# LayerNorm's channel sums in a decoder block: GpSimd in place of TensorE, with six pairs of weight low parts on VectorE

## The chip, the core and the metric

The kernel runs on one core of a Trainium2 chip. The metric is device time in microseconds (us); three runs of the kernel before gave 786.52, 786.67 and 786.81 us.

The core has five engines, each working through a queue of its own in order: TensorE (PE in the profile; PEld is its weight load), VectorE (DVE), ScalarE (ACT), GpSimd (POOL) and SyncE (SP, which here only starts DMA transfers). They wait for each other through semaphores.

## The reference

One decoder block, batch 1, 512 positions, 1024 channels, float32. Two token mixers run side by side and a SwiGLU channel mixer follows. The part that matters here is the convolution branch with its LayerNorm, and what stands beside it:

```python
def layernorm(x, g, b):
    mu = jnp.mean(xf, axis=-1, keepdims=True)
    xc = xf - mu
    var = jnp.mean(xc * xc, axis=-1, keepdims=True)
    return xc * lax.rsqrt(var + EPS) * g + b
...
z_glu, z_rx, z_rg, z_ga, z_gb = jnp.split(h @ w_in[l] + b_in[l], split_idx, axis=-1)
u = z_glu[..., :D_CONV] * jax.nn.sigmoid(z_glu[..., D_CONV:])
u = causal_depthwise_conv(u, conv_dw_w[l], conv_dw_b[l])          # 31 taps
u = jax.nn.silu(layernorm(u, conv_ln_g[l], conv_ln_b[l]))
y_a = u @ conv_w_out[l] + conv_b_out[l]
...
y_b = (hb * jax.nn.gelu(z_rg, approximate=True)) @ lru_w_out[l]
m = jax.nn.sigmoid(z_ga) * y_a + jax.nn.sigmoid(z_gb) * y_b
x = x + m @ w_mix_out[l]
```

LayerNorm needs two sums over the 1024 channels for each of the 512 positions: one for the mean, one for the variance.

## The kernel before, in words

**Layout and products.** Activations lie channel by channel on the 128 partitions with the 512 positions along the row, so 1024 channels are 8 tiles of 128x512. A product of float32 matrices is made from two parts of each operand: a high part in the narrower type `fp32r` (a cast on ACT, line 126) and a low part, the rest (a subtraction, line 122). `mm3` (line 621) adds high x high, high x low and low x high, so that each weight tile costs three matmuls.

**Weights.** `wchunk` lists the weight pieces in the order in which PE wants them. A piece is loaded by SP into one of 8 raw buffers, cast by ACT, and its low part is made by the engine named by the argument `lo`: GpSimd (`pool_e`) by default, VectorE (`vec`) for some. High and low part go into one of 5 buffers (`hl`), which come free when PE is done with the piece five places earlier. The matrix `lru_w_out` comes as 16 pieces of 128x640, two for each of 8 output tiles (`lo0_0`, `lo0_1`, up to `lo7_1`); all low parts of these are on GpSimd. PE uses them in the stage that I call the `yb` stage (8 output tiles, 30 matmuls each), after the products with `w_in` (`z`) and ahead of those with `conv_w_out` (`ya`, which reads the normalised `un0` to `un7`).

**Order.** Most of the program is in the engines' queues in an order that the code writes itself (`tc.manual_schedule`). Small steps of VectorE work are dealt out beside the matmuls: generators such as `conv_lane` (the 31 taps, line 874) and `conv_norm` (LayerNorm) yield after each step, and `run_beside` takes so many steps of them for each output tile of PE. `MEAN_LAG` and `LAG` are counts of such steps that `conv_norm` lets pass between the two halves of a sum, so that the engines that make it have time.

**LayerNorm before.** The convolution lanes add the 8 tiles into `lnmt` (line 879). `conv_norm` splits this into a high part (`lnmsh`, ACT) and a low part (`lnmsl`, VectorE). `column_mean` (line 891) multiplies each by a 128x128 matrix of ones on PE, which leaves the sum over partitions on all partitions, and ACT scales it (line 892, `lnmp`, in PSUM). VectorE subtracts it from the 8 tiles (`u<-u,lnmp`), ACT squares them (line 906), VectorE adds the squares into `lnvt` (line 909, in PSUM), and the same split and products follow (`lnvsh`, `lnvsl`, `lnvp`). ACT takes the root (line 916), VectorE the reciprocal (line 917), then 8 products `u<-u,lnvp` (line 921), Silu on ACT (line 923), and the split into `un`.

**Other work in that place.** `mixq.make_sums` (tiles `mxws`, lines 113 and 344) prepares sums of quarters of `w_mix_out` on VectorE. `make_f_sums` does the same for pieces of the feed-forward weights: 12 pieces (`fws`), each loaded, added up by four GpSimd additions (line 114) and stored to DRAM (line 442, from GpSimd's queue for the last four).

Of the kernel before, what the change touches and what calls it, by code (L numbers as in the profile page):

```python
# [1 line left out]

# [5 lines left out]

# [2 lines left out]
AF = mybir.ActivationFunctionType  # L11
ALU = mybir.AluOpType

P = 128
T = 512
D = 1024
DC = 1024
# [20 lines left out]
PACK = HB // 2  # L38
ROWS_G = HB + PACK

MEAN_LAG, LAG = 9, 7
LANE_IN, LANE_OUT, XB_LAG, STEP_ROOM, LOAD_AHEAD, GATE_LAG = 3, 0, 1, 8.3, 2, 2


# [11 lines left out]
SUMS_AT, SUMS_STEP, SUMS_LAG, STORE_LAG = 3, 5, 2, 2  # L56
STORED_LAG = 3
SUMS_OWN = 40


MIX_LATE_LAG, LATE_LAG = 2, 8
# [23 lines left out]
def tile_block(ctx, tc, a, out):  # L85
# [8 lines left out]
    def tiles(tag, bufs):  # L94
        p_ = pool(tag, bufs)
        return lambda name, dtype=F32: p_.tile([P, T], dtype, tag=tag, name=name)

    longt, shortt = tiles("long", SLOTS), tiles("short", SHORT)

    def pairt(name, dtype=F32R):  # L100

        return longt(f"{name}h", dtype), longt(f"{name}l", dtype)

    def bank(name):
        return psum.tile([P, T], F32, tag="mm", name=name)

    def bank2(name):
        return psum2.tile([P, T], F32, tag="cv", name=name)

    vec, act, pe, pool_e = nc.vector, nc.scalar, nc.tensor, nc.gpsimd  # L110
# [5 lines left out]
    newest = {}  # L116
# [4 lines left out]
    def sub(eng, o, x, y):  # L121
        return eng.tensor_tensor(out=o, in0=x, in1=y, op=ALU.subtract)  # L122

    def split_to(h, l, full, eng, copy=act.copy):

        copy(h, full)  # L126
        if eng is None:
            put_off.append((l, full, h.bitcast(F32)))
            return h, l
        last = sub(eng, l, full, h.bitcast(F32))  # L130
        newest["sub" if eng is pool_e else "low"] = last.ins
        return h, l
# [17 lines left out]
    def split(name, full, eng, p_=None, copy=act.copy):  # L150
        p_ = p_ or pairt(name)
        return split_to(*p_, full, eng, copy)
# [7 lines left out]
    def wchunk(key, src, kt, cols, where="hl", lo=pool_e, after=None):  # L160
        chunks.append((key, src, kt, cols, where, lo, after))
# [87 lines left out]
    ORDER = """u0 u1 rx0 rx1 gb0 rx2 u2 gb1 h0 rx3 h1 h2 u3 rx4 h3 u4 h4 gb2 h5 rx5 h6 rg0 rx6 h7 u5 rx7 h8 gb3 rg1 rg2 rx8 h9 h10 rg3 gb4 u6 h11 rx9 h12 u7 h13 gb5 rg4 rg5 rg6 ga0 gb6 h14 ga1 gb7 ga2 rg7 h15 ga3 rg8 ga4 ga5 rg9 ga6 ga7""".split()  # L249
    ORDER = [(t.rstrip("0123456789"), int(t.lstrip("abcdefghijklmnopqrstuvwxyz"))) for t in ORDER]  # L250
# [9 lines left out]
    lru_out = a["lru_w_out"][0].rearrange("(k p) n -> p k n", p=P)  # L260
    for j in range(8):
        for hf in range(2):
            wchunk(f"lo{j}_{hf}", lru_out[:, 5 * hf : 5 * hf + 5, j * P : (j + 1) * P], 5, P)
    conv_out = a["conv_w_out"][0].rearrange("(k p) n -> p k n", p=P)
    for j in [0, 4, 1, 5, 2, 6, 3, 7]:
        wchunk(f"co{j}", conv_out[:, :, j * P : (j + 1) * P], ND, P, lo=vec)
# [158 lines left out]
    def piece_load(name, halves, queue=nc.sync):  # L425
        raw = raws.tile([P, 1024], F32, tag="raw", name=f"fws{name}")
        n = 1024 // len(halves)
        for h, src in enumerate(halves):
            queue.dma_start(raw[:, h * n : h * n + n].rearrange("p (e n) -> p e n", n=256), src)
        return raw  # L430

    def piece_sums(raw, dest, eng):
        of = raw.rearrange("p (h k e n) -> p h e k n", h=2, k=2, e=2)
        q11, q12, q21, q22 = (of[:, h, e] for h in range(2) for e in range(2))
        plus_on(eng, q22, q22, q12)
        plus_on(eng, q12, q12, q11)
        plus_on(eng, q11, q22, q11)
        plus_on(eng, q21, q21, q11)

    def piece_store(raw, dest, queue=nc.sync):  # L440
        dest = dest.rearrange("p m k n -> p (m k) n")
        return queue.dma_start(dest, raw.rearrange("p (m n) -> p m n", n=256))

    def make_f_sums():

        todo = list(f_todo)  # L450
        sums_due, stores_due = [], []
        n, next_at, stored = 0, SUMS_AT, [-9]
        while todo or sums_due or stores_due:
            if stores_due and (emitted[0] >= stores_due[0][0] or not (todo or sums_due)):
                stores_due.pop(0)[1]()
                stored[0] = n
            if sums_due and n >= sums_due[0][0]:
                sums_due.pop(0)[1]()
            if todo and n >= next_at and len(sums_due) + len(stores_due) + (n < stored[0] + STORED_LAG) < PIECES:
                next_at += SUMS_STEP  # L460
                name, halves, dest = todo.pop(0)
                with tc.issue_after(newest["load"]):
                    raw = piece_load(name, halves)

                def sums(raw=raw, dest=dest, own=n >= SUMS_OWN):
                    with tc.issue_after(newest["sub"]):
                        piece_sums(raw, dest, pool_e)
                        if own:
                            piece_store(raw, dest, pool_e)
                            return  # L470

                    def stores():
                        with tc.issue_after(newest["load"]):
                            piece_store(raw, dest)

                    stores_due.append((emitted[0] + STORE_LAG, stores))

                sums_due.append((n + SUMS_LAG, sums))
            n += 1
            yield  # L480
# [90 lines left out]
    eps_t = consts.tile([P, 1], F32, name="eps_t")  # L571
# [11 lines left out]
    onesr = consts.tile([P, P], F32R, name="onesr")  # L583
# [24 lines left out]
    def pc(name, i):  # L608
        return par[:, col[name] + i : col[name] + i + 1]
# [249 lines left out]
    ended, total = [], []  # L859
# [24 lines left out]
            act.copy(u[c], acc)  # L884
            yield False

    def column_mean(name, tot, scale):

        ps = bank2(f"{name}p")
        for i, v in enumerate(tot):  # L890
            pe.matmul(ps, onesr, v, start=i == 0, stop=i == 1)  # L891
        act.activation(ps, ps, AF.Copy, scale=scale)
        return ps

    def conv_norm():
        tot = split("lnms", total[0], vec)
        yield True
        for _ in range(MEAN_LAG):
            yield True
        mean = column_mean("lnm", tot, 1.0 / DC)  # L900
        yield True
        tot = bank2("lnvt")
        for c in range(8):
            sub(vec, u[c], u[c], mean)
            q = tot if c == 0 else shortt(f"sq{c}")
            act.activation(q, u[c], AF.Square)
            yield True
            if c:
                vec.tensor_tensor(out=tot, in0=tot, in1=q, op=ALU.add)
                yield True  # L910
        tot = split("lnvs", tot, vec)
        yield True
        for _ in range(LAG):
            yield True
        rs = column_mean("lnv", tot, 1.0 / DC)
        act.activation(rs, rs, AF.Sqrt, bias=eps_t)
        vec.reciprocal(rs, rs)
        for _ in range(6):
            yield True
        for c in range(8):  # L920
            vec.tensor_tensor(out=u[c], in0=u[c], in1=rs, op=ALU.mult)
            yield True
            act.activation(u[c], u[c], AF.Silu, scale=pc("conv_ln_g", c), bias=pc("conv_ln_b", c))
            un.append(split(f"un{c}", u[c], vec))
            yield True

    lanes += [conv_lane(0), conv_lane(1)]
    norm = conv_norm()

    def beside_one():  # L930
# [254 lines left out]
    for j in range(8):  # L1185
        ws = w_tiles(f"lo{j}_0", 5) + w_tiles(f"lo{j}_1", 5)
        ps = bank(f"yb{j}")
# [123 lines left out]
    for n, j in enumerate(mixq.order()):  # L1311
        ws = w_tiles(f"co{j}", ND)
        ps = bank(f"ya{j}")
# [424 lines left out]
```

## Time and profile before

| what | value |
|---|---|
| runs | 786.52, 786.67, 786.81 us (median 786.67) |
| profiled execution, its own time | 786.66 us |
| its span, first to last instruction | 784.7 us, so 1.96 us lie around it |
| mean granted TensorE clock | 0.998 |
| busy: PE, DVE, ACT, POOL | 778.4, 662.8, 476.1, 277.8 us |
| `yb` stage: PE starts it, PE starts `ya` | 310.70 us, 365.63 us |

A row of the timeline reads: start in us from the span's first instruction, duration in us, engine, source line, operation, output<-inputs (buffer numbers left out), shape, count, and in brackets the idle time of that engine just before, with what ended it. A PE row's duration is longer than the distance to the next row's start, because matmuls overlap; the distance is what a matmul costs. In the chain of work that ended last, each piece is what the end of the program waited for at that time.

### The profile page before, as it was taken

The numbers are of one execution on the slowest core, as the hardware profiler recorded it, in microseconds if no ns is written. First come the engines' busy times: TensorE is split into PE (matmuls) and PEld (weight loads), VectorE is DVE, ScalarE is ACT, GpSimd is POOL, SyncE is SP. The second block draws the span as 40 slices with busy tenths as digits, with TensorE's granted clock in tenths as the row PEclk, the third lists the DMA queues.
The fourth block names the chain that finished last, engine by engine and source line by source line (L and its number), as shares of the span: only waits on it lengthen the run. The fifth ranks groups of instructions, "written<-read, shape, count | busy, mean of one in ns | idle before, by whom it ended". The sixth has DMA issues, their size and how long they took to land.

```text
span 784.7 us, 12214 instructions
## 1 busy us (share of the span) xinstructions
PE 778.4 (99%) x4329; PEld 680.9 (87%) x4329; DVE 662.8 (84%) x993; ACT 476.1 (61%) x699; POOL 277.8 (35%) x223
## 2 busy tenths in 40 slices
PE   9999999999999999999999999999999999999997
PEld 9988888888888888888888898999999999888886
DVE  6389998898987995999867869779888889999957
ACT  8443778976785687565224676555554555666844
POOL 4366857577556655730000361312212220000001
PEclk9999999999999999999999999999999999999999
DMA  8827978697793553558665466997989794679522
GB/s 246 232 58 211 252 213 233 164 260 213 205 250 117 162 170 96 199 176 266 219 195 163 151 235 210 231 303 208 270 235 241 252 213 141 212 238 297 172 67 108
DMA packets 181198, 158.64 MB, mean 202 GB/s; under 512 B 14202, under 2 KB 146450, under 8 KB 181138
## 3 DMA queue, kind: packets, MB, share of 16 engines
q1 hardware_dynamic: 171186, 132.43, 58.2%
q0 software_dynamic: 9792, 25.17, 13.0%
q8 instruction: 34, 0.56, 0.3%
q14 instruction: 26, 0.21, 0.1%
q10 hardware_dynamic: 160, 0.27, 0.1%
HBM read 132.14 MB, written 35.65 MB: 214 GB/s over the span
## 4 chain that ended last, share of the span: by engine, by line
PE 99%; ACT 0%; DVE 0%; issue 0%
PE z L621 36%; PE fr L1443 25%; PE or L1248 13%; PE yb L621 7%; PE ya L621 6%; PE mxr L1248 5%; PE f L621 3%; PE g L1074 2%; PE fr L1506 1%; PE warm L590 1%; PE tx L682 0%; PE th L666 0%; PE z L739 0%; ACT of L1680 0%; PE orl L1248 0%; PE lnvp L891 0%
## 5 line engine op out<-in xcount | busy, mean ns | idle before, releaser
L874 DVE SCALAR_TENSOR_TENSOR cv<-u,par,cv 128x507 f32<-128x507 f32 (+15 forms) x240 | 162.2, 735 | 4.2 <-ACT cv L870 3.3
L122 POOL TENSOR_TENSOR hl_in<-raw_in,hl_in 128x1024 fp32r<-128x1024 f32 (+1 forms) x52 | 122.8, 2371 | 87.2 <-ACT hl_in L126 83.2
L1443 PE MATMUL fr<-hs_0h,hl_ft 128*128 128x256 f32 x320 | 59.2, 283 | 0.0
L126 ACT CAST hl_in<-raw_in 128x1024 fp32r<-128x1024 f32 x50 | 51.5, 1048 | 1.5 <-PE z L621 0.8
L1443 PEld LDWEIGHTS fr<-hs_0h,hl_ft 128*128 128x128 f32 x320 | 50.6, 192 | 0.0
L487 POOL DMA_DIRECT2D ot<-in_ffn_w_dram x24 | 26.4, 1110 | 54.2 <-DVE hl_ft L122 32.8
L122 POOL TENSOR_TENSOR hl_ot<-raw_ot,hl_ot 128x1024 fp32r<-128x1024 f32 x1 | 2.4, 2412 | 121.3 <-ACT hl_ot L126 121.3
L126 ACT CAST hl_fb<-raw_fb 128x1024 fp32r<-128x1024 f32 x30 | 31.3, 1048 | 23.1 <-PE fr L1443 10.9
L1443 PE MATMUL fr<-hs_0l,hl_ft 128*128 128x256 f32 x160 | 45.3, 283 | 0.0
L122 DVE TENSOR_TENSOR hl_fb<-raw_fb,hl_fb 128x1024 fp32r<-128x1024 f32 x29 | 35.4, 1222 | 10.3 <-ACT hl_fb L126 9.8
L621 PE MATMUL z<-h10h,hl_in 128*128 128x512 f32 (+1 forms) x108 | 41.1, 382 | 0.0
L621 PE MATMUL z<-h12h,hl_in 128*128 128x512 f32 (+1 forms) x108 | 40.8, 379 | 0.0
L621 PE MATMUL z<-h13h,hl_in 128*128 128x512 f32 (+1 forms) x108 | 40.8, 379 | 0.0
L621 PE MATMUL z<-h14h,hl_in 128*128 128x512 f32 (+1 forms) x108 | 40.8, 379 | 0.0
L621 PE MATMUL z<-h15h,hl_in 128*128 128x512 f32 (+1 forms) x108 | 40.8, 379 | 0.0
L621 PE MATMUL z<-h16h,hl_in 128*128 128x512 f32 (+1 forms) x108 | 40.8, 379 | 0.0
L621 PE MATMUL z<-h11h,hl_in 128*128 128x512 f32 (+1 forms) x108 | 40.8, 379 | 0.0
L621 PE MATMUL z<-h17h,hl_in 128*128 128x512 f32 (+1 forms) x108 | 40.8, 379 | 0.0
L114 POOL TENSOR_TENSOR fws<-fws 128x256 f32<-128x256 f32 x48 | 37.1, 773 | 2.7
L126 ACT CAST hl_ft<-raw_fb 128x1024 fp32r<-128x1024 f32 x28 | 28.6, 1050 | 14.7 <-DVE raw_fb L113 11.8
L122 POOL TENSOR_TENSOR hl_lo<-raw_lo,hl_lo 128x640 fp32r<-128x640 f32 x16 | 26.7, 1680 | 26.8 <-ACT hl_lo L126 26.8
L126 ACT CAST hl_ob<-raw_ob 128x1024 fp32r<-128x1024 f32 (+1 forms) x23 | 23.4, 1016 | 21.0 <-PE or L1248 14.7
(957 smaller groups left out, 2610.2 us busy)
## 6 DMA issues: line engine op xcount, KB each, us to landing
raw_in<-in_w_in_dram SPq DMA_DIRECT2D x51, 512.0 KB
raw_fb<-in_ffn_w_dram SPq DMA_DIRECT2D x74, 256.0 KB
ot<-in_ffn_w_dram POOLq DMA_DIRECT2D x30, 512.0 KB, 8.3
raw_ob<-in_ffn_w_dram SPq DMA_DIRECT2D x33, 256.0 KB
raw_ot<-ot SPq DMA_DIRECT2D x33, 256.0 KB
fws<-in_ffn_w_dram SPq DMA_DIRECT2D x12, 512.0 KB
raw_lo<-in_lru_w_out_dram SPq DMA_DIRECT2D x16, 320.0 KB
ot<-ot POOLq DMA_DIRECT2D x10, 512.0 KB, 6.2
```

Source lines behind the costliest of these rows:

```text
L114: plus_on = lambda eng, o, x, y: eng.tensor_tensor(out=o, in0=x, in1=y, op=ALU.add)
L122: return eng.tensor_tensor(out=o, in0=x, in1=y, op=ALU.subtract)
L126: copy(h, full)
L487: plus = lambda o, x: pool_e.dma_start(o, x, accum_op=ALU.add)
L590: pe.matmul(wp[:, :P], ones, ones, start=True, stop=True)
L621: pe.matmul(ps, l, r, start=i == 0, stop=i == n - 1)
L874: vec.scalar_tensor_tensor(out=acc[:, s:], in0=u[c][:, : T - s], scalar=dw(c, s), in1=acc[:, s:], op0=ALU.mult, op1=ALU.add)
L1074: pe.matmul(ps[:HB], head_chunk[0][:ROWS_G, g, h % 2, m, :], ext[h][m][:ROWS_G], start=m == 0, stop=m == 1)
L1248: pe.matmul(banks[i][:, cs], l_[:, ts], r_[:, cs], start=start and n == 0, stop=stop and n == 2, skip_group_check=again)
L1443: pe.matmul(ps[:, HALVES[i]], lw[:, c, :], rx_, start=not (again or i or c or m), stop=bool(i and c == 3 and m == 2), skip_group_check=True,)
L1506: pe.matmul(self.r4[:, HALVES[i]], lw, rx_, start=not (i or c or m), stop=bool(i and c == 3 and m == 2), skip_group_check=True)
```

## The change

`column_mean` goes. In its place `column_sums` issues one GpSimd operation, `partition_all_reduce`, which reads a 128x512 tile and writes the sum over all partitions to each partition of another 128x512 tile. It is used twice, for the mean and for the variance. The splits of the two totals go with the products. `lnvt` moves from PSUM to SBUF. The scaling goes into the ACT instruction that follows. The lags between the halves become 12 and 9 steps.

The low parts of `lo0_0` to `lo5_1` (twelve subtractions) go from GpSimd to VectorE. In `make_f_sums`, the pieces that come due after the ordered list is through are added up by VectorE and no longer held back behind GpSimd's newest low part; this is one piece, `fws3_1_1`. Its store stays in GpSimd's queue.

```diff
-MEAN_LAG, LAG = 9, 7
+MEAN_LAG, LAG = 12, 9
+LO_BY_DVE = 6
-            wchunk(f"lo{j}_{hf}", lru_out[:, 5 * hf : 5 * hf + 5, j * P : (j + 1) * P], 5, P)
+            wchunk(f"lo{j}_{hf}", lru_out[:, 5 * hf : 5 * hf + 5, j * P : (j + 1) * P], 5, P, lo=vec if j < LO_BY_DVE else pool_e)
-                    with tc.issue_after(newest["sub"]):
-                        piece_sums(raw, dest, pool_e)
+                    with tc.issue_after(newest["sub"]) if n < len(ORDER) else nullcontext():
+                        piece_sums(raw, dest, pool_e if n < len(ORDER) else vec)
-    def column_mean(name, tot, scale):
-        ps = bank2(f"{name}p")
-        for i, v in enumerate(tot):
-            pe.matmul(ps, onesr, v, start=i == 0, stop=i == 1)
-        act.activation(ps, ps, AF.Copy, scale=scale)
-        return ps
+    def column_sums(name, tot):
+        sums = longt(name)
+        pool_e.partition_all_reduce(sums, tot, P, bass_isa.ReduceOp.add)
+        return sums
     def conv_norm():
-        tot = split("lnms", total[0], vec)
+        mean = bank2("lnmp")
+        sums = column_sums("lnms", total[0])
...
-        mean = column_mean("lnm", tot, 1.0 / DC)
+        act.activation(mean, sums, AF.Copy, scale=1.0 / DC)
         yield True
-        tot = bank2("lnvt")
+        tot = longt("lnvt")
...
-        tot = split("lnvs", tot, vec)
+        sums = column_sums("lnvs", tot)
...
-        rs = column_mean("lnv", tot, 1.0 / DC)
-        act.activation(rs, rs, AF.Sqrt, bias=eps_t)
+        rs = bank2("lnvp")
+        act.activation(rs, sums, AF.Sqrt, scale=1.0 / DC, bias=eps_t)
         vec.reciprocal(rs, rs)
```

The queues show what that moves. GpSimd from its last `w_in` low part to the feed-forward pieces, before:

```order
L122 TENSOR_TENSOR hl_in43_2985<-raw_in43_2880,hl_in43_2985 128x1024
L122 TENSOR_TENSOR hl_lo0_0_3029<-raw_lo0_0_2923,hl_lo0_0_3029 128x640
L122 TENSOR_TENSOR hl_lo0_1_3067<-raw_lo0_1_2965,hl_lo0_1_3067 128x640
...
L122 TENSOR_TENSOR hl_lo2_1_3124<-raw_lo2_1_3122,hl_lo2_1_3124 128x640
L114 TENSOR_TENSOR fws3_1_1_3032<-fws3_1_1_3032 128x2x128 x4
L442 DMA fs3_82<-fws3_1_1_3032 128x4x256
L122 TENSOR_TENSOR hl_lo3_0_3181<-raw_lo3_0_3179,hl_lo3_0_3181 128x640
...
L122 TENSOR_TENSOR hl_lo7_1_3434<-raw_lo7_1_3432,hl_lo7_1_3434 128x640
```

The same place in GpSimd's queue now; the two rows named only `ISA` change GpSimd's code library, to the one that holds the reduction and back:

```order
L123 TENSOR_TENSOR hl_in43_2985<-raw_in43_2880,hl_in43_2985 128x1024
L443 DMA fs3_82<-fws3_1_1_3031 128x4x256
L891 ISA
L891 ISA lnms_3024<-lnmt_1069 128x512
L891 ISA lnvs_3268<-lnvt_3148 128x512
L123 ISA
L123 TENSOR_TENSOR hl_lo6_0_3335<-raw_lo6_0_3333,hl_lo6_0_3335 128x640
L123 TENSOR_TENSOR hl_lo6_1_3340<-raw_lo6_1_3338,hl_lo6_1_3340 128x640
L123 TENSOR_TENSOR hl_lo7_0_3407<-raw_lo7_0_3405,hl_lo7_0_3407 128x640
L123 TENSOR_TENSOR hl_lo7_1_3412<-raw_lo7_1_3410,hl_lo7_1_3412 128x640
```

Twelve low parts and one piece's additions left this queue, and between the two reductions GpSimd does nothing else.

VectorE from the last step of the recurrent branch to the first additions of squares, before:

```order
L122 TENSOR_TENSOR y9l_3064<-z35_2988,y9h_3063 128x512
L122 TENSOR_TENSOR u0_500<-u0_500,lnmp_3102 128x512
L122 TENSOR_TENSOR u1_519<-u1_519,lnmp_3102 128x512
L122 TENSOR_TENSOR u2_878<-u2_878,lnmp_3102 128x512
L122 TENSOR_TENSOR u3_1130<-u3_1130,lnmp_3102 128x512
L909 TENSOR_TENSOR lnvt_3106<-lnvt_3106,sq1_3112 128x512
```

The same place now:

```order
L123 TENSOR_TENSOR y9l_3063<-z35_2988,y9h_3062 128x512
L123 TENSOR_TENSOR hl_lo0_1_3066<-raw_lo0_1_2965,hl_lo0_1_3066 128x640
L123 TENSOR_TENSOR hl_lo1_0_3098<-raw_lo1_0_3013,hl_lo1_0_3098 128x640
L123 TENSOR_TENSOR hl_lo1_1_3105<-raw_lo1_1_3058,hl_lo1_1_3105 128x640
L123 TENSOR_TENSOR u0_500<-u0_500,lnmp_3023 128x512
L123 TENSOR_TENSOR hl_lo2_0_3108<-raw_lo2_0_3094,hl_lo2_0_3108 128x640
L123 TENSOR_TENSOR u1_519<-u1_519,lnmp_3023 128x512
L123 TENSOR_TENSOR u2_878<-u2_878,lnmp_3023 128x512
L123 TENSOR_TENSOR u3_1130<-u3_1130,lnmp_3023 128x512
L909 TENSOR_TENSOR lnvt_3148<-lnvt_3148,sq1_3152 128x512
```

Three low parts now stand ahead of the first wait for the mean, and the rest stand between LayerNorm's steps, behind that wait.

VectorE again, around the reciprocal of the second sum, now (before, eight `mxws` and `mxt` steps, two `sgb` steps and `lnvsl` stood between the last `lnvt` addition and the reciprocal, line 917, and no low part of a weight behind it):

```order
L909 TENSOR_TENSOR lnvt_3148<-lnvt_3148,sq7_3223 128x512
L123 TENSOR_TENSOR hl_lo4_0_3227<-raw_lo4_0_3225,hl_lo4_0_3227 128x640
L114 TENSOR_TENSOR mxws0_1_3271<-mxws0_1_3271,mxws0_0_3270 128x512
L114 TENSOR_TENSOR mxws0_0_3270<-mxws0_0_3270 128x512
L114 TENSOR_TENSOR mxws0_0_3270<-mxws0_1_3271,mxws0_0_3270 128x512
L917 RECIPROCAL lnvp_3330<-lnvp_3330 128x512
L123 TENSOR_TENSOR hl_lo4_1_3232<-raw_lo4_1_3230,hl_lo4_1_3232 128x640
```

The low part of `lo4_1`, which PE needs for the second half of `yb4`, now stands behind the reciprocal. ACT's queue has moved likewise: `lnmp` (now line 900) comes right behind `sga7`, which reads the last `z` product, and the cast of `lo2_0` behind it; the root `lnvp` comes behind the cast of `lo4_0`, and the cast of `lo4_1` behind the root. On PE only the four products with ones are gone (two ahead of `yb0`, two ahead of `yb3`).

More of the change, by code (lines that the diff above doesn't have):

```diff
@@ L4 @@
 import concourse.tile as tile
-from concourse import mybir
+from concourse import bass_isa, mybir
 from concourse.masks import make_identity
```

## The prediction

> **What bounds the kernel now.** I read the profile's page first, then the chain of work that ended last around the `yb` stage, then the timelines of each engine there. The page's head, its busy times and its chain:
>
> ```profile
> span 784.7 us, 12214 instructions
> PE 778.4 (99%) x4329; PEld 680.9 (87%) x4329; DVE 662.8 (84%) x993; ACT 476.1 (61%) x699; POOL 277.8 (35%) x223
> PE 99%; ACT 0%; DVE 0%; issue 0%
> ```
>
> TensorE works from end to end; no other engine has a share of the chain worth a per cent. So the change can gain only what it takes off PE's queue, and lose only where PE comes to wait. The chain's pieces in the stage concerned (start, length, what, matmuls):
>
> ```profile
> 310.40 0.47 PE lnmp L891 x2
> 310.87 20.43 PE yb L621 x90
> 331.29 0.47 PE lnvp L891 x2
> 331.76 34.03 PE yb L621 x150
> 365.79 6.35 PE ya L621 x28
> ```
>
> The four products with ones cost 0.47 + 0.47 = 0.94 us, and nothing waits in between: 34.03/150 = 0.227 us a matmul, one `yb` tile of 30 is 6.81 us. PE's own timeline at the first pair:
>
> ```profile
> 310.01 0.39 PE L621 MATMUL z<-h17h,hl_in 128*128 128x512 f32 x1
> 310.24 0.40 PE L891 MATMUL lnmp<-lnmsh,onesr 128*128 128x512 f32 x1
> 310.47 0.39 PE L891 MATMUL lnmp<-lnmsl,onesr 128*128 128x512 f32 x1
> 310.70 0.39 PE L621 MATMUL yb<-y0h,hl_lo 128*128 128x512 f32 x1
> ```
>
> From 310.24 to 310.70 is 0.46 us, which I take for each pair with 0.47 for the second: **0.93 us** gained. With the change `yb0` starts at 310.24, `yb4` at 337.5, and the second half of `yb4` (15 matmuls on) at 340.9.
>
> **The two unknowns.** No row of before shows the reduction (D us, twice) or the change of code library (L us, once ahead of the first reduction, once behind the second). GpSimd's nearest rows, the load of ACT's function tables, and a GpSimd-queue transfer's landing (last number of its row):
>
> ```profile
> L122 POOL TENSOR_TENSOR xb9l<-xb,xb9h 128x512 fp32r<-128x512 f32 x1 | 1.3, 1294 | 0.0
> 289.01 1.28 ACT L1125 ACT_TABLE_LOAD   x1
> ot<-in_ffn_w_dram POOLq DMA_DIRECT2D x30, 512.0 KB, 8.3
> ```
>
> D: one pass of GpSimd over 128x512 is 1.29 us; that is the lower end. If 128 partitions are added by seven halvings, each as dear as a whole pass, D is 9.0 us; that is my upper end. I take four passes, 5.2 us, the middle, since the later halvings carry less data. L: at least a table load, 1.3 us; at most a large transfer, 8.3 us; I take the middle, 4.8 us. Neither can be below zero, and an early result gains nothing, because PE doesn't wait for it today.
>
> [...]
>
> **First sum: when is it there, when is it wanted?** The rows of VectorE and ACT around it:
>
> ```profile
> 297.45 0.69 DVE L879 TENSOR_TENSOR lnmt<-lnmt,cv 128x512 f32<-128x512 f32 x1
> 303.31 0.69 DVE L122 TENSOR_TENSOR y9l<-z,y9h 128x512 fp32r<-128x512 f32 x1 [0.65 <-ACT y9h L1144]
> 311.73 2.48 DVE L122 TENSOR_TENSOR u<-u,lnmp 128x512 f32<-128x512 f32 x4 [7.72 <-ACT lnmp L892]
> 324.81 0.69 DVE L909 TENSOR_TENSOR lnvt<-lnvt,sq 128x512 f32<-128x512 f32 x1
> 312.99 0.67 ACT L1125 ACTIVATE sga<-z,par 128x512 f32<-128x512 f32 x1
> L113 DVE TENSOR_TENSOR mxu<-sga,sgb x8: 420/425/426, 373.5 to 410.1; 128x256 f32<-128x256 f32 x8
> 287.51 0.77 POOL L442 DMA_DIRECT2D fs<-fws  x1 [0.30 <-DMA raw_lo<-in_lru_w_out_dram]
> ```
>
> `lnmt` ended at 298.14. Four `fws` additions of 128x256 (0.42 us each by the row of that shape) now stand ahead of it: 1.7 us, so 299.8. They end about two steps sooner, near 298.5; GpSimd then issues the store (0.77 us) and starts the library change at 299.3. The sum is there at 299.3 + L + D = 309.3. ACT now makes `sga7` ahead of `lnmp`, which needs the last `z` product (about 310.4) and 0.67 us: `lnmp` can't start before 311.1 anyhow, and VectorE's first subtraction not before 311.7, where it starts today. So L + D is free up to 311.1 - 299.3 = 11.8; at 10.0 the first wait costs nothing. Behind `lnmp` on ACT wait the cast of `lo2_0`, behind `u0` on VectorE its low part; PE wants them at 323.9 (`yb2`), 12 us later.
>
> **VectorE's added work.** Twelve low parts of 128x640. The neighbours in size, VectorE's low part of `co` and the reciprocal's surroundings:
>
> ```profile
> L122 DVE TENSOR_TENSOR hl_co<-raw_co,hl_co x8: 1212/1217/1223, 359.8 to 383.6; 128x1024 fp32r<-128x1024 f32 x8
> 315.41 0.69 DVE L909 TENSOR_TENSOR lnvt<-lnvt,sq 128x512 f32<-128x512 f32 x1
> 316.01 0.68 DVE L122 TENSOR_TENSOR u<-u,lnmp 128x512 f32<-128x512 f32 x1
> 334.67 0.69 DVE L113 TENSOR_TENSOR mxws<-mxws,mxws 128x512 f32<-128x512 f32 x1 [2.67 <-DMA mxws<-in_w_mix_out_dram]
> 339.18 3.36 DVE L917 RECIPROCAL lnvp<-lnvp 128x512 f32<-128x512 f32 x1
> 360.90 0.68 DVE L122 TENSOR_TENSOR un7l<-u,un7h 128x512 fp32r<-128x512 f32 x1
> L621 PEld LDWEIGHTS ya<-un7h,hl_co x16: 187/188/188, 370.2 to 408.7; 128*128 128x128 f32 x16
> ```
>
> Between 0.69 (512) and 1.22 (1024) a low part of 640 takes 0.82 us; steps of 512 follow each other every 0.60 us (315.41 to 316.01), so one of 640 takes 0.73 of the queue. Twelve are 8.8 us and the additions 1.7; `lnmsl` and `lnvsl` save 1.4: 9.1 us more. Two idle times of VectorE cover it, 7.72 + 2.67 = 10.4 us. The cover's end is `un7`: its low part ended at 361.6 and PE loads it at 370.2, or 369.3 with the 0.93 us gained, so 7.7 us are spare even there.
>
> **Second sum.** From `u0` to the last `lnvt` addition VectorE's queue now has 17 steps at 0.60 and four low parts at 0.73: 13.1 us from 311.7, or the wait for `yb1` (30 x 2 matmuls from 310.24 are 323.9) and two steps: 325.3 at the latest. This is where it ended before (325.5). So the second sum is there at 325.4 + 5.2 = 330.6. Then follow the root (0.66 by the row below), the reciprocal (3.36) and, new behind it, the low part of `lo4_1` (0.82): 4.9 us with the steps between, 335.5. PE wants that on the third matmul of `yb4`'s second half, at 341.3:
>
> ```profile
> 333.90 0.66 ACT L916 ACTIVATE lnvp<-lnvp,eps_t 128x512 f32<-128x512 f32 x1
> ```
>
> Spare: 5.8 us. This is the tightest place: PE waits once D, plus what the first sum came late, exceeds 11.0. Both sums together are hidden while L + 2D stays under 11.8 + 11.0 = **22.8 us**; I have 15.2. At the upper ends, 8.3 + 18.0 = 26.3, PE loses 3.5. Later the second library change delays `lo6_0` on GpSimd to 335.4 + 1.6; PE wants it at 351, so it is covered by 14 us.
>
> **GpSimd holding VectorE.** Two pairs of rows that lie beside each other:
>
> ```profile
> 288.30 2.41 POOL L122 TENSOR_TENSOR hl_in<-raw_in,hl_in 128x1024 fp32r<-128x1024 f32 x1
> 288.89 2.37 DVE L968 SCALAR_TENSOR_TENSOR xb<-th,xb 128x512 f32<-128x512 f32 x1
> 321.23 3.10 POOL L122 TENSOR_TENSOR hl_lo<-raw_lo,hl_lo 128x640 fp32r<-128x640 f32 x2
> 321.40 3.49 DVE L113 TENSOR_TENSOR mxws<-mxws 128x512 f32<-128x512 f32 x1
> ```
>
> A VectorE step of 0.69 us became 2.37 and 3.49: it ended about 0.55 us behind GpSimd's work (290.71, 324.33). The `lnvt` step at 315.41, with one operand in PSUM, kept 0.69 beside a GpSimd low part. [...] If a reduction holds VectorE for all its length, `lo0_1` to `lo1_1` (about 2.4 us with their gaps) are left behind the first sum, where `u0` needs it at 309.3, and `lo4_0` and three `mxws` steps (2.5, against 0.7 otherwise) behind the second: cover falls to 10.0 + 9.2 = 19.2 us. My 15.2 still fits, with 4.0 spare; the upper ends would cost 7.1. On the other side GpSimd's twelve low parts no longer hold VectorE.
>
> **Sum.** 786.66 - 0.93 = 785.73 us for the profiled execution; the median of the runs, 786.67, is 0.01 above it, so **785.7**. That is 0.12% less. About 0.2%, 1.6 us, is what a measurement of this kernel can tell from no change, so the forecast is "within 0.2%".
>
> **Rivals.**
>
> *The reduction is longer than its cover.* It pays at one place, the low part of `lo4_1` behind the reciprocal, from L + 2D = 22.8 on (19.2 if it holds VectorE), one for one. Slower by over 0.2% means a loss of 2.5 us or more: L + 2D over 25.3 (21.7). At the upper ends it gives 785.73 + 3.5 = 789.2, with VectorE held 792.8. For it: the ends of D and L reach there; the waits are real, since both reductions are in series with VectorE. Against it: GpSimd's row of 1.29 us a pass. Chance 0.15.
>
> *It works column by column.* The smallest GpSimd instruction is this:
>
> ```profile
> 0.24 0.10 POOL L1724 MEMSET const-float32-0.0<- 128x1 f32 x1 [0.24 <-issue]
> ```
>
> If each of the 512 columns costs one such step, D is 51 us, L + 2D = 107, PE waits 84 us, and the time is about 870. Against it: a pass of 512 columns takes 1.29 us, 2.5 ns a column. Chance 0.07. [...]
>
> *More than 0.94 us comes off.* Faster by 1.6 us needs a PE wait that goes away, and the chain shows none in this stage; a last term could only come from GpSimd no longer holding VectorE, and PE doesn't wait for VectorE. Chance 0.03.
>
> **How the numbers follow.** The forecast has 0.75, a loss of up to 2.5 us from a sum that just overruns included; slower 0.15 + 0.07 = 0.22; faster 0.03. The range starts at 785.4 (the run spread, 0.3, below the forecast) and ends at 789.3, the upper ends of both unknowns without the holding; beyond lie the rest of the first rival and the second, together under 2 in 10.
>
> **What would show it.** Right: PE's rows go from `z` to `yb` to `yb` to `ya` without a gap; no L891 on PE; the reduction's two rows well under 9 us; `u<-u,lnmp` starts near 311.7, the reciprocal near 331. Wrong: a PE wait at `yb4`'s second half with the low part of `lo4_1` (VectorE) as releaser, a wait of `u0` on `lnmp` long after 312, or VectorE's low parts stretched as long as the reduction runs and PE waiting for `lo0_1` or `lo1_0`.

## The result, and the profile after

The changed kernel takes **785.57 us** (median of 22 runs, 785.19 to 785.86); the kernel before, run beside it, took 786.90 us (22 runs, 786.52 to 788.53). The ratio is 0.998, 95% interval 0.9974 to 0.9987 (the two medians alone give 0.9983). The forecast was 785.7 with a range of 785.4 to 789.3, so the time is where it was put, but the forecast called it "no change". The interval reaches 0.07% to each side and lies clear of 1: it is a small gain.

The head of the page, the busy times and the chain's shares, after:

```profile
span 784.0 us, 12205 instructions
PE 776.4 (99%) x4325; PEld 679.2 (87%) x4325; DVE 667.9 (85%) x1007; ACT 473.8 (60%) x696; POOL 262.5 (33%) x209
PE 98%; DMA 1%; DVE 0%; ACT 0%; SPq 0%; issue 0%
```

PE has four matmuls fewer and 2.0 us less busy time. 1.1 us of that lie in the first 25 us, far ahead of the change, where PE's start differs from run to run; so the busy time does not measure the gain. The chain around the `yb` stage, which had five pieces before, now has three:

```profile
299.96 10.65 PE z L622 x47
310.61 54.40 PE yb L622 x240
365.01 7.03 PE ya L622 x31
```

All 240 `yb` matmuls stand in one piece. Before they were 20.43 + 34.03 = 54.46 us in two, so the two interruptions cost the 0.94 us of the products and another 0.06.

GpSimd's timeline in the same place, and the row of the instruction that changes the library, from the view of line 891 (durations in ns, then first and last start):

```profile
L891 POOLq MODIFY_POOL_CONFIG  x2: 37/37/37, 299.2 to 299.3; - x2
```

```profile
298.45 0.77 POOL L443 DMA_DIRECT2D fs<-fws  x1 [0.58 <-DVE fws L115]
304.92 3.75 POOL L891 PARTITION_ALL_REDUCE lnms<-lnmt  x1 [5.70 <-DVE y9l L123]
325.72 3.65 POOL L891 PARTITION_ALL_REDUCE lnvs<-lnvt  x1 [17.05 <-DVE lnvt L909]
340.39 1.56 POOL L123 TENSOR_TENSOR hl_lo<-raw_lo,hl_lo 128x640 fp32r<-128x640 f32 x1 [11.02 <-ACT hl_lo L127]
```

The library change is asked for at 299.3 and the reduction begins at 304.92: L = 5.6 us. The releaser named, `y9l`, is nothing that the reduction reads: in the program its one wait on VectorE is for the last `lnmt` addition, and that was done at 299.5 (next fence). The releaser is an inference of the profile; beside the two rows of 37 ns it shows nothing of what the 5.6 us are. D is 3.75 and 3.65 us, the whole sum over 128 partitions.

VectorE, at the places that the prediction put times on:

```profile
298.82 0.69 DVE L880 TENSOR_TENSOR lnmt<-lnmt,cv 128x512 f32<-128x512 f32 x1
...
311.86 0.69 DVE L123 TENSOR_TENSOR u<-u,lnmp 128x512 f32<-128x512 f32 x1 [2.79 <-ACT lnmp L900]
...
324.86 0.69 DVE L909 TENSOR_TENSOR lnvt<-lnvt,sq 128x512 f32<-128x512 f32 x1
...
326.19 2.73 DVE L114 TENSOR_TENSOR mxws<-mxws,mxws 128x512 f32<-128x512 f32 x1
...
330.29 3.36 DVE L917 RECIPROCAL lnvp<-lnvp 128x512 f32<-128x512 f32 x1
333.56 0.81 DVE L123 TENSOR_TENSOR hl_lo<-raw_lo,hl_lo 128x640 fp32r<-128x640 f32 x1
```

`lnmt` ends at 299.51 (forecast 299.8), `u0` starts at 311.86 (311.7), the last `lnvt` ends at 325.55 (325.3), the reciprocal starts at 330.29 (331), the low part of `lo4_1` ends at 334.37 (335.5), where PE wants it at about 341.5.

**A ruler finer than the median.** The start differs from run to run: in the changed kernel the chain's first pieces hang on the landing of the first load (`x<-in_x_dram`, 4.81 us of the chain). So I measure each profiled execution from the end of the `par_ps` transposes (on PE, 23 us into the span) to the start of the last piece of `or` (PE's last products). The two pieces of before, of after, and of two experiments (e3, e8) that are told below, from their chains:

```profile
22.65 0.44 PE par_ps L602 x4
...
778.74 0.72 PE or L1248 x6
```

```profile
22.86 0.44 PE par_ps L603 x4
...
777.96 0.72 PE or L1248 x6
```

```profile
23.07 0.44 PE par_ps L603 x4
...
779.13 0.72 PE or L1250 x6
```

```profile
22.75 0.44 PE par_ps L603 x4
...
778.33 0.73 PE or L1250 x6
```

| kernel | start of the last `or` piece, less end of `par_ps` |
|---|---|
| before; before again (e1) | 755.65; 755.65 |
| low parts moved alone (e2) | 755.65 |
| after; after again (e9) | 754.66; 754.66 |
| after, four products put back (e3) | 755.62 |
| after, variance summed by two products (e8) | 755.14 |
| reduction issued twice (e4); five pairs moved (e11) | 754.66; 754.65 |
| thrice (e5); four times (e6); four pairs moved (e10) | 760.32; 765.06; 760.99 |

One kernel gives the same number to 0.02 us in two executions. By this ruler the change gains **0.99 us**.

### The profile page after: what moved, and what is told of

It reads as the page before. It is cut to its first block, busy times and chain, and to the rows that moved or that the text cites. A ratio compares the mean times of both kernels' runs of the same rounds, so it can differ in the third digit from the quotient of the medians.

```text
span 784.0 us, 12205 instructions
## 1 busy us (share of the span) xinstructions
PE 776.4 (99%) x4325; PEld 679.2 (87%) x4325; DVE 667.9 (85%) x1007; ACT 473.8 (60%) x696; POOL 262.5 (33%) x209
## 4 chain that ended last, share of the span: by engine, by line
PE 98%; DMA 1%; DVE 0%; ACT 0%; SPq 0%; issue 0%
PE z L622 36%; PE fr L1443 25%; PE or L1248 13%; PE yb L622 7%; PE ya L622 6%; PE mxr L1248 5%; PE f L622 3%; PE g L1074 2%; PE fr L1506 1%; DMA x<-in_x_dram 1%; PE tx L683 0%; PE th L667 0%; PE z L740 0%; ACT of L1680 0%; PE orl L1248 0%; DVE n1j L704 0%
## 5 line engine op out<-in xcount | busy, mean ns | idle before, releaser
L115 POOL TENSOR_TENSOR fws<-fws 128x256 f32<-128x256 f32 x44 | 34.1, 774 | 2.4
L123 DVE TENSOR_TENSOR hl_ft<-raw_fb,hl_ft 128x1024 fp32r<-128x1024 f32 x28 | 33.6, 1218 | 1.2 <-ACT hl_ft L127 1.2
```

The costliest lines, as they stand in the source:

```text
L115: plus_on = lambda eng, o, x, y: eng.tensor_tensor(out=o, in0=x, in1=y, op=ALU.add)
```

## The experiments

The theory is that of the prediction: the four products are the whole gain, and the two reductions are hidden up to the place behind the reciprocal. The rivals are that the gain comes from moving low parts off GpSimd, and that the cover ends somewhere else than the prediction put it.

**e1: the kernel before against itself.** No edit.

> The kernel before, timed against itself, to see how far two sets of runs of one program differ. Both theories: ratio 1.000. If the two medians differ by about 0.4 us, the part of the measured gain above the 0.94 us of the four products is within what two sets of runs differ by; if they agree within 0.1 us, it is not.

786.81 (11 runs) against 786.75 (33 runs), ratio 1.0001, interval 0.9992 to 1.001. So eleven runs against thirty-three tell apart about 0.09%, 0.7 us, less than half of what the prediction took for the least that can be told.

**e2: the low parts alone.** The kernel before, with the second half of the change only:

```diff
+LO_BY_DVE = 6
...
-            wchunk(f"lo{j}_{hf}", ..., 5, P)
+            wchunk(f"lo{j}_{hf}", ..., 5, P, lo=vec if j < LO_BY_DVE else pool_e)
...
-                    with tc.issue_after(newest["sub"]):
-                        piece_sums(raw, dest, pool_e)
+                    with tc.issue_after(newest["sub"]) if n < len(ORDER) else nullcontext():
+                        piece_sums(raw, dest, pool_e if n < len(ORDER) else vec)
```

> Only the low parts of lo0_0 to lo5_1 and one piece's additions go to VectorE; both sums stay products with ones on TensorE. Theory 'products' (the gain is the four products and nothing else): the time of before, 0.0 +- 0.2 us, PE still without a gap. Theory 'second gain' (GpSimd's relief also takes off about 0.4 us somewhere): 0.4 us below before.

786.58 (11 runs) against 786.75 (33 runs), ratio 0.9998, interval 0.9989 to 1.0007; by the ruler exactly the kernel before. Inside the span, moving them gains nothing by itself.

**e3: the products put back.** The changed kernel, with four products with ones ahead of `lnmp`. They write the PSUM tile that ACT's scaling overwrites, so that only PE's time for them comes back:

```diff
+        for v in h1p[0] + h1p[1]:
+            pe.matmul(mean, onesr, v, start=True, stop=True)
         act.activation(mean, sums, ...)
```

> The kernel after with four products with ones put back on TensorE ahead of yb0 (on other operands, their result is overwritten by the scaled sum). Theory 'products': 4 x 0.23 = 0.9 us above the kernel after and level with before. Theory 'second gain': 0.9 us above the kernel after too, but still 0.4 us below before.

786.65 (11 runs) against 786.75 (33 runs), ratio 0.9997, interval 0.9988 to 1.0005. Its chain:

```profile
310.82 0.93 PE lnmp L901 x4
311.76 54.43 PE yb L622 x240
```

0.93 for the products and 0.03 more in `yb` are 0.96, what the ruler shows (755.62 - 754.66). The gain is gone, with all else of the change still there.

**e8: half of it.** The changed kernel, with the variance summed by split and products as before; the mean stays on GpSimd:

```diff
-        sums = column_sums("lnvs", tot)
+        tot = split("lnvs", tot, vec)
-        act.activation(rs, sums, AF.Sqrt, ...)
+        for i, v in enumerate(tot):
+            pe.matmul(rs, onesr, v, start=i == 0, stop=i == 1)
+        act.activation(rs, rs, AF.Sqrt, ...)
```

> The kernel after with the variance's sum made by two products with ones as before, the mean's by GpSimd. Theory 'products': half the gain, 0.47 us above the kernel after, 0.5 us below before; counted from the end of the first transposes to PE's last products, where runs agree within 0.05 us, half way between the two kernels. Theory 'second gain': nearer to the kernel after, since the low parts are moved here too.

786.09 (11 runs) against 786.95 (15 runs), ratio 0.999, interval 0.9981 to 0.9999: between the two kernels. By the ruler it is half the gain (755.14 - 754.66 = 0.48 of 0.99).

```profile
310.50 27.20 PE yb L622 x120
337.70 0.47 PE lnvp L917 x2
338.16 27.23 PE yb L622 x120
```

Two products are 0.47, the interruption 0.03 (27.20 + 27.23 against 54.40), together 0.50 for the ruler's 0.48. So the products account for the ruler's gain to within 0.02 us.

**e4, e5, e6: where the cover ends.** The reduction issued two, three, four times over, from the same input into the same output:

```diff
-        pool_e.partition_all_reduce(sums, tot, P, bass_isa.ReduceOp.add)
+        for _ in range(2):     # e5: 3, e6: 4
+            pool_e.partition_all_reduce(sums, tot, P, bass_isa.ReduceOp.add)
```

> The kernel after with each reduction issued twice in a row, so that each sum takes 2 x 3.7 = 7.4 us in place of 3.7. The prediction's cover, by the measured start (304.9, since the library change took 5.6 us): the first sum is there at 312.3, 1.1 us late; the second at 326.8 + 7.4 = 334.2, its low part of lo4_1 at 339.1, against 341.3 wanted. Theory 'cover of 11 us at the second sum': no loss, the time of the kernel after within 0.2 us. Rival 'the reductions lie on the path': up to 7.4 us slower.

785.61 (11 runs), ratio 0.9984, interval 0.9975 to 0.9993, and 754.66 by the ruler: 7.4 us of further GpSimd work cost nothing. GpSimd and VectorE of e4:

```profile
304.75 7.11 POOL L892 PARTITION_ALL_REDUCE lnms<-lnmt  x2 [5.85 <-DVE y9l L123]
326.02 7.64 POOL L892 PARTITION_ALL_REDUCE lnvs<-lnvt  x2 [14.16 <-DVE lnvt L910]
```

```profile
327.23 2.62 DVE L114 TENSOR_TENSOR mxws<-mxws 128x512 f32<-128x512 f32 x1
329.88 3.34 DVE L114 TENSOR_TENSOR mxws<-mxws,mxws 128x512 f32<-128x512 f32 x2
334.42 3.37 DVE L918 RECIPROCAL lnvp<-lnvp 128x512 f32<-128x512 f32 x1 [1.20 <-ACT lnvp L917]
337.69 0.81 DVE L123 TENSOR_TENSOR hl_lo<-raw_lo,hl_lo 128x640 fp32r<-128x640 f32 x1
```

The low part of `lo4_1` ends at 338.5, 2.7 us ahead of its use at about 341.2. VectorE now waits for the sum (1.20), which it did not in the changed kernel.

> The kernel after with each reduction issued three times. In the run with two, the second sum's low part of lo4_1 ended at 338.5 and PE wanted it at 341.3 to 341.4; a third reduction adds about 3.6 at the mean and 3.7 at the variance, so it ends near 345.8: PE waits 4.4 us there and nowhere else. Theory 'cover': 785.6 + 4.4 = 790.0 us, the wait at the second half of yb4 with VectorE's low part as its cause. Rival 'the reductions are hidden however long': 785.6.

791.58 (4 runs) against 786.95 (15 runs), ratio 1.0062, interval 1.0049 to 1.0076. PE's timeline in the middle of `yb4`, and two rows of the windows (bounds, length, busy time of PE, PEld, DVE, ACT and POOL, granted clock, DMA share, GB/s):

```profile
341.86 0.50 PE L622 MATMUL yb<-y5h,hl_lo 128*128 128x512 f32 x1 [0.85 <-ACT hl_lo L127]
342.20 0.40 PE L622 MATMUL yb<-y5l,hl_lo 128*128 128x512 f32 x1
345.33 0.79 PE L622 MATMUL yb<-y5h,hl_lo 128*128 128x512 f32 x1 [2.74 <-DVE hl_lo L123]
345.93 0.63 PE L622 MATMUL yb<-y6h,hl_lo 128*128 128x512 f32 x1
346.35 0.63 PE L622 MATMUL yb<-y6l,hl_lo 128*128 128x512 f32 x1
```

```profile
344.00:348.00 4.00, 2.67 (x6) 2.15 (x7) 4.00 (x7) 1.39 (x2) 0.00 (x0) 0.64 0.42 126
348.00:352.00 4.00, 4.00 (x18) 3.23 (x17) 4.00 (x7) 2.83 (x5) 1.30 (x1) 0.93 0.89 260
```

The wait is at the third matmul of `yb4`'s second half, for the low part of `lo4_1` on VectorE: the place, the tile and the releaser that the prediction named. PE went on at 345.33 instead of 341.3, 4.0 us late (4.4 expected). One part was not foreseen: the *high* part is late too (0.85 us), since its cast stands on ACT behind the root, which waits for the sum. The other 1.6 us of the 5.66 by the ruler are the clock: from 345.93 on the matmuls start 0.42 us apart instead of 0.227, with a granted clock of 0.64 in that window and 0.93 in the next.

> Each reduction four times. Theory 'cover': past the edge each further reduction at both sums costs its full length twice, 3.6 + 3.7 = 7.3 us above the run with three: 797.3 us. Rival 'PE's wait is shared with other slack': less than 5 us above the run with three.

797.38 (4 runs), ratio 1.0132, interval 1.0118 to 1.0146. The total is as expected, but not for the reason given. PE waits in other places:

```profile
349.11 0.80 PE L622 MATMUL yb<-y0h,hl_lo 128*128 128x512 f32 x1 [4.67 <-ACT hl_lo L127]
...
353.25 0.80 PE L622 MATMUL yb<-y0h,hl_lo 128*128 128x512 f32 x1 [2.92 <-DVE hl_lo L123]
```

These are the two parts of the next piece, `lo5_0`. With the longer reduction the order that is written out puts the low part of `lo4_1` *ahead* of the reciprocal on VectorE:

```
e5:  437 L918 RECIPROCAL lnvp     438 L123 TENSOR_TENSOR hl_lo4_1     441 L123 TENSOR_TENSOR hl_lo5_0
e6:  436 L123 TENSOR_TENSOR hl_lo4_1     439 L918 RECIPROCAL lnvp     442 L123 TENSOR_TENSOR hl_lo5_0
```

So the cover of e6 ends at another tile, some 3 us later, and one long spell of half clock over both waits makes up for it (granted clock 0.84, 0.50, 0.50 and 0.88 in the four windows of 4 us from 344 to 360, 10.2 us at half). e6 does not test "one for one".

**e7, e10, e11: how many low parts must move.** The changed kernel with `LO_BY_DVE` at 0, 4 and 5.

> The kernel after with all low parts of lo left on GpSimd (LO_BY_DVE = 0); the queue then has the library change, the mean's reduction, the change back, lo0_0 to lo2_1, the change, the variance's reduction, the change back, and the rest. Theory 'a library change of 5.6 us on either side holds the low parts': lo0_0's low part is there at 308.7 + 5.6 + 1.6 = 315.9 in place of 310.7 (PE waits 5.2 us), lo3_0's at about 338 in place of 336 (2 us): about 792.8 us. Rival 'moving the low parts was not needed': 785.6.

801.41 (4 runs), ratio 1.0188, interval 1.0172 to 1.0203. GpSimd in e7, and what PE waited for:

```profile
304.95 3.25 POOL L891 PARTITION_ALL_REDUCE lnms<-lnmt  x1 [5.86 <-DVE y9l L123]
314.98 11.38 POOL L123 TENSOR_TENSOR hl_lo<-raw_lo,hl_lo 128x640 fp32r<-128x640 f32 x6 [6.78 <-ACT sq L906]
332.60 3.25 POOL L891 PARTITION_ALL_REDUCE lnvs<-lnvt  x1 [6.23 <-DVE mxt40l L123]
343.20 9.58 POOL L123 TENSOR_TENSOR hl_lo<-raw_lo,hl_lo 128x640 fp32r<-128x640 f32 x6 [7.36 <-ACT un0h L127]
```

```profile
PE yb L622 <- POOL hl_lo L123: 9.0, 2, 5.6
```

Four library changes instead of two. The way back, from a reduction's end to the next low part, takes 6.8 and 7.4 us, and PE waits behind both. The mechanism was as expected; the size was not (792.8 expected), because I left out the half clock after each wait (granted clock 0.50 from 316 to 320 and from 344 to 348) and because six low parts took 11.38 us, 1.9 each, beside VectorE's work.

> LO_BY_DVE is 4 instead of 6: the low parts of lo4_0 to lo5_1 stay on GpSimd, behind the second reduction and the change of library back. Theory (GpSimd's way back takes 6.8 to 7.4 us from a reduction's end to its next low part): the second reduction ends near 329.4, the next low part starts at 336.2 to 336.8 and takes 1.6 to 1.9, so lo4_0 is there at 337.8 to 338.7; PE wants it on the third matmul of yb4, at 337.9. PE waits 0 to 0.8 us, 785.6 to 786.4 in all, ratio 0.9985 to 0.9995, and the named releaser is the low part of lo4_0 on POOL. Rival (the twelve moved low parts are more than the change needs and cost VectorE time that PE later waits for): no wait on POOL, and the time is below that of the changed kernel by 0.2 us or more.

791.75 (5 runs) against 786.71 (15 runs), ratio 1.0059, interval 1.0045 to 1.0073. Both expectations missed. GpSimd's timeline:

```profile
304.94 3.60 POOL L891 PARTITION_ALL_REDUCE lnms<-lnmt  x1 [5.85 <-DMA raw_lo<-in_lru_w_out_dram]
324.98 1.85 POOL L123 TENSOR_TENSOR hl_lo<-raw_lo,hl_lo 128x640 fp32r<-128x640 f32 x1 [16.44 <-ACT hl_lo L127]
333.91 3.25 POOL L891 PARTITION_ALL_REDUCE lnvs<-lnvt  x1 [7.08 <-issue]
344.59 10.05 POOL L123 TENSOR_TENSOR hl_lo<-raw_lo,hl_lo 128x640 fp32r<-128x640 f32 x6 [7.43 <-ACT hl_lo L127]
```

I had put all four pairs' low parts behind the second reduction. GpSimd's order has `lo4_0` between the two, since its buffer comes free in time. That one instruction of 1.85 us sends the library back and forth: the second reduction starts at 333.91 instead of 325.72, and `lo4_1` is there at 346.1 where PE wanted it at 341.4 (a wait of 4.65 us in PE's row).

> LO_BY_DVE is 5: the low parts of lo5_0 and lo5_1 stay on GpSimd, and in GpSimd's order they stand behind the second reduction, so that the library changes no more often than in the changed kernel. Theory (with four pairs moved the loss came only from lo4_0, which stood between the two reductions and cost a change back and a second change): the second reduction ends near 329.4, the way back takes about 7, lo5_0 is there at 338.1 and PE wants it at 344.7; no wait, 785.6 us, ratio 0.9983 to 0.9987, aligned time 754.66. Rival (GpSimd's way back with three pairs waiting behind it is itself too long, whatever stands between the reductions): a PE wait on a low part of POOL, 786.5 us or more.

785.51 (11 runs) against 786.91 (15 runs), ratio 0.9984, interval 0.9975 to 0.9993, and 754.65 by the ruler. Without `lo4_0` in between, two more low parts on GpSimd cost nothing:

```profile
325.45 3.65 POOL L891 PARTITION_ALL_REDUCE lnvs<-lnvt  x1 [17.04 <-DVE lnvt L909]
337.04 5.54 POOL L123 TENSOR_TENSOR hl_lo<-raw_lo,hl_lo 128x640 fp32r<-128x640 f32 x3 [7.93 <-ACT hl_lo L127]
```

Five pairs do as well as six; the difference to the changed kernel is within both intervals. Of the counts tried (0, 4, 5 and 6), those that lose are the ones that leave a low part between the two reductions.

**e9: the changed kernel again.** No edit.

> The changed kernel once more, unaltered, beside the kernel before. Theory (the four products with ones are the whole gain, 1.00 us by the aligned traces): 1.00 us less than before, ratio 0.9987, and the chain from the end of the par_ps transposes to the first matmul of the last or piece is 754.66 us again. Rival (something besides the products has become quicker, since the first medians differ by 1.33 us): ratio 0.998 again, 1.3 us or more, with an aligned time under 754.5.

785.62 (11 runs) against 786.71 (15 runs), ratio 0.9983, interval 0.9975 to 0.9992; 1.09 us in medians, 0.99 by the ruler: the ratio lies between what the two theories expected, the ruler's number is the theory's.

## Why the prediction was right, and where it failed

- **What the products cost.** Forecast 0.93, measured 0.99 by the ruler: the products' 0.94 and 0.03 for each of the two places where the `yb` sequence was broken. e3 and e8 carry it: the gain comes and goes with the products, 0.48 for two, 0.96 for four in one place.
- **The rest of the medians' difference.** 786.90 - 785.57 is 1.33. The time of a run less its span is on average 1.93 to 2.04 us in every set of runs of the kernel before (1.97 in e1) and 1.99 in e7, where no low part moved; it is 1.76 to 1.80 in the changed kernel, in e2, and in all others that moved four to six pairs. So 0.2 us go with the move of the low parts, and lie outside the first and last instruction, where no row shows what they are: that cause stays open. The last 0.1 is within what the start varies by.
- **The step that failed** is the one that made the class of the sum: "About 0.2%, 1.6 us, is what a measurement of this kernel can tell from no change, so the forecast is 'within 0.2%'". No run stood behind that 0.2%; the 22 runs tell 0.07%, a third of it, so the 0.12% less that the sum gave was already a gain to be told. The sum itself was too small by two terms, 0.06 for the breaks and 0.2 around the span, which carried the medians to 1.33 us or 0.17% less. That the time is so near the 785.7 forecast is in part luck: the median of before beside it was 786.90, 0.2 above the one that the sum started from. The prediction had priced "More than 0.94 us comes off" at 0.03, and named as its only way a VectorE freed from GpSimd; e2 shows that this way brought nothing inside the span.
- **D, the reduction.** Taken 5.2 from the middle of 1.29 and 9.0; measured 3.75 and 3.65 in the changed kernel, 3.23 to 4.27 over all runs, and 3.25 in e7, where VectorE did next to nothing beside it: under the value taken, 2.5 to 3.3 passes of GpSimd over the tile. So the column-by-column rival (51 us) is out.
- **L, the change of library.** Taken 4.8; the idle times ahead of the reductions are 5.70 here, 5.85 in e4, 5.86 and 6.23 in e7, 7.08 for e10's second. The changed kernel's second reduction, with no change ahead of it, began 0.17 us behind the last `lnvt` addition (325.55 to 325.72). The way back is dearer: 6.8 and 7.4 in e7, and at most 7.4 in e10 and 7.9 in e11, where the low part's own cast on ACT ended only 0.46 us ahead of it.
- **The two covers.** The first: `u0` starts at 311.86, as forecast, because `sga7` stands ahead of `lnmp`. The second: L and both sums take 5.6 + 3.75 + 3.65 = 13.0 now, some 20.5 in e4 (2.7 us to spare) and 27.2 in e5 (4.0 us late). Both put the edge at 23.2. The forecast was 22.8 with VectorE free, 19.2 with VectorE held all the time. The tile, the matmul and the releaser were those named.
- **VectorE held.** Forecast as a bound, and it is real: the `mxws` step that began 0.5 us into the second reduction took 2.73 us instead of 0.69. The holding is paid out of the time in which VectorE would have waited for the sum, so the cover did not shrink as the lower figure supposed.
- **Moving the low parts.** Forecast as nothing gained and 9.1 us of VectorE work hidden; e2 shows 0.00 by the ruler. That they *must* move was not worked out in the prediction. e7 and e10 show it: 15.8 and 6.2 us slower than the changed kernel.

## What to carry to other kernels

The instruction that needed another code library on GpSimd cost here its own 3.2 to 4.3 us and, for the way there and back, 12.6 and 13.6 us (5.86 + 6.78 and 6.23 + 7.36 in e7); group such instructions, and look in GpSimd's order for anything that stands between two of them. Beside a PE that never waited, taking work off PE gained that work to within 0.1 us, and work on the other engines counted only once it passed its cover; issuing the new operation twice and three times finds that edge. Before you call a small forecast "no change", work out the interval that the runs would have: with eleven runs or more it was here under 0.1%.

## What the runs showed of the hardware

- **A long PE wait cost more than itself.** After waits of 2.74 us (e5), 4.65 (e10), 4.67 and 2.92 (e6, one spell) and 3.44 and 5.56 (e7) the matmuls ran at half the clock until PE had worked some 3 to 5 us. In e5 these were seven matmuls from 345.33 to 348.49, 0.42 us apart or more, 1.6 us lost; the granted clock was 0.72 and 0.85 in e10's two windows of 4 us from 344 to 352, 0.50 and 0.77 in e7's from 316 to 324, 0.50 and 0.86 in e7's from 344 to 352. In e5 the clock did not wait for PE to go on: the two windows (0.64 and 0.93 of 4 us each) put the half clock from about 345.1 to 348.6, an estimate with one spell at half and full clock otherwise. That begins about 2.5 us into the wait of 2.74 (342.59 to 345.33). Ahead of that wait PE had worked 0.73 us, from 341.86 on, since the wait of 0.85; behind the wait of 0.85 the next matmul still followed after 0.34 us. Whether the wait of 2.74 us alone would have been enough is not shown.
- **The reduction held an `mxws` step of VectorE for most of its length, not all.** In the changed kernel the held `mxws` step ended at 328.92, 0.45 us before the reduction (329.37). In e4 the held `mxws` step ended at 329.85; of the two behind it, 3.34 us together and each 0.69 when free, the second was through at 333.22, 0.44 us before the repetition beside them ended (333.66).
- **A break in a run of matmuls** cost PE 0.03 us beside the matmuls that make it (54.46, 54.43 and 54.40 us for the same 240 with two, one and no break).
